# Where the FFN's order starts and ends: weight splits, down units and the final norm moved in the instruction order of a one-core encoder step

## The chip, the core and the metric

The program runs on one core of one Trainium2 chip. Its engines work at the same time and each takes its own instructions in order: PE multiplies matrices, with its weight loads shown apart as PEld; DVE works elementwise; ACT copies, scales and applies functions; POOL is a slower third elementwise engine; and SP's queue issues most of the transfers. The metric is the device time of one execution in microseconds; the median of three runs before is 843.84 us (840.65 to 845.9).

## What is computed

One layer of a hybrid encoder over a token block of 544 columns: 32 sample tokens, then 512 prompt tokens (meta tokens are dropped before this part). After the attention branches:

```
h = h + einsum('btd,de->bte', m, w_out)
u = einsum('btd,df->btf', rmsnorm(h, norm_ffn), w_up)      # 1024 -> 4096
h = h + einsum('btf,fd->btd', square(relu(u)), w_down)     # 4096 -> 1024
y = rmsnorm(h, norm_final)
```

The work this case is about lies between the product with `w_out` and the output of `y`: the feed-forward network (FFN), from about 443 us to the end.

## The kernel before

**Values in two parts.** Every operand of a large product is split into a high part (rounded by ACT, line 121) and a low part (the rest, subtracted by DVE, line 124), and a product is three matmuls: high with high, high with low, low with high. Names ending in `h` or `hi` are high parts, in `l` or `lo` low parts (`whi`/`wlo`, `hh`/`hl`, `uh`/`ul`, `dh`/`dl`, `lh`/`ll`).

**The up products (`up_pair`, line 1365).** The 4096 rows of u are made in 16 pairs of 128. A pair is a 2x2 block product over halves of the 1024 inputs and halves of the 544 tokens, done with seven products of 12 matmuls (128x272) in place of eight. In order they take the weights a11, s1, s2, s4, s3, a12, a22 (the s are sums and differences of blocks, made by DVE from the raw `wr`) and the operand combinations B11, BM, BN, B22, BT3, B21, BT4 in `hh`/`hl`. They accumulate in three PSUM tiles, `ps_x`, `ps_v` and `ps_y`, and ACT copies a partial result out (`fa`, `fb`, `x`) before the next product adds to the same tile, so that product waits for the copy. `up_pair` is a generator with seven steps, n = 0 to 6; the program does other work between its steps. `pair_prep` (line 263) is the generator that loads and splits a pair's weights, one step ahead; pair 0 is prepared while the last two `w_out` products run.

**The operands (`operands`, line 1231).** The eight 128-row parts d of h come out of the `w_out` loop in the order 0, 4, 1, 5, 2, 6, 3, 7 (line 1272): DVE adds the product to `xres`, ACT and DVE scale it, combine the halves and split into `hh`/`hl`. The last part's combinations (`b`, `bb`, `ba`) are what the third product of pair 0 waits for.

**The down products (`down`, line 1441).** The up pairs are grouped into eight chunks, `CHUNKS`, of 1, 2, 2, 2, 2, 2, 2 and 3 pairs. For every chunk c there are eight units d: 128 rows of the output times the chunk's u, in two column ranges of 288 and 256 tokens (`OC`). The units of chunk c-1 are put between the steps n = 1, 3, 5, 6 of the first two pairs of chunk c (lines 1492 to 1503). Their weights are loaded into `dr` and split by `down_prep` (line 326). Chunk 0's results are copied to `acc` by ACT; `square` (line 1472) adds up the squares of h, and `norm2` (line 1481) makes the FFN norm's factor `r2` from them with two small matmuls `ps_r`.

**The last chunk (lines 1509 to 1554).** Chunk 7 has 18 matmuls per unit and column range. The eight units run over the first 288 columns, then over the last 256. Units 0 and 1 use the `whi`/`wlo` buffers that the up weights used before, units 2 to 7 new ones (`lh`/`ll`). `last_evac` multiplies by `r2` (`dt`) and adds to `hs` (`xres`). `final_part` (line 1313) transposes h on PE (`ps_fin`), squares it on ACT (`fj`) and multiplies by the norm's weight on DVE (`ytok`); T0 is the first three token tiles, T1 the last two, and the parts 0, 1, 2 cover d = 0 to 3, 4 to 6 and 7. `final_norm` scales the rows and sends them out.

**What sets the order.** From line 1205 on PE, ACT and DVE run their instructions in the order in which the program's source issues them. SP's and POOL's order is chosen by a scheduler. A buffer of a pool is given to its next tile when the last reader of the former tile is done.

Of the kernel before, what the change touches and what calls it, by code (L numbers as in the profile page):

```python
# [15 lines left out]
P = 128  # L16
# [31 lines left out]
def tile_hybrid_step(  # L48
# [185 lines left out]
    def unit_prep(n):  # L234
        key, parts = units[n]
        raw = wpool.tile([P, KD, P], F32, tag="raw", name=f"wr_{n}", bufs=3)
        k = 0
        for src in parts:
            kk = src.shape[0] // P
            SP.dma_start(raw[:, k: k + kk, :], src.rearrange("(k p) n -> p k n", p=P))  # L240
            k += kk
        if parts[0].shape[0] == D and key[0] in IN_KEYS:
            POOL.tensor_tensor(raw, raw, gmix.unsqueeze(2).to_broadcast([P, KD, P]), ALU.mult)  # L243
        hi = wpool.tile([P, KD, P], F32R, tag="whi", name=f"wh_{n}", bufs=2)
        lo = wpool.tile([P, KD, P], F32R, tag="wlo", name=f"wl_{n}", bufs=2)
        split_hi(hi, raw)
        split_lo(lo, raw, hi)
        done[key] = (hi, lo)
# [14 lines left out]
    def pair_prep(g):  # L263
# [47 lines left out]
        if g == 0:  # L311
            for i, nm in enumerate(("s2", "s4")):
                split(one(nm), 0, [nm], s24[:, i: i + 1])
        else:
            B = t(wpool, "whi", bufs=2), t(wpool, "wlo", bufs=2)
            split(B, 0, ["s2", "s4"], s24)
# [955 lines left out]
    for n, d in enumerate(WO_ORDER):  # L1272
        xr = tmp([TM], f"xres{d}")
        POOL.tensor_tensor(xr, xh[:, d, M0:].bitcast(F32), xl[:, d, M0:].bitcast(F32), ALU.add)
        wh, wl = use(("wo", d))
        if n == KD - 2:
            prep = pair_prep(0)
            go(prep, 3)
        if n == KD - 1:
            go(prep, 4)  # L1280

        def evac_o(ci, a, b, ps, xr=xr):
            DVE.tensor_tensor(xr[:, a:b], ps, xr[:, a:b], ALU.add)

        blocks(f"wo{d}", range(KD), wh, wl, lambda k, a, b: mh[k][:, a:b], lambda k, a, b: ml[k][:, a:b],
               OC, evac_o, psany, both=n == 0)
        hs[d] = xr
        operands(d, n == KD - 1)
# [76 lines left out]
    def up_pair(g):  # L1365
# [13 lines left out]
        if g == 0:  # L1379
# [3 lines left out]
            drain(own)  # L1383
# [6 lines left out]
        ACT.activation(fb[:, 1, :], vv, AF.Copy)  # L1390
        yield
        product(X, W["s2"], BN, False)
        ACT.activation(fa[:, 1, :], xv, AF.Copy)
        go(prep, 1)
# [46 lines left out]
    def down(i):  # L1441
        c, d = dn[i]
        if i + 1 < len(dn):
            go(dpreps[i + 1], 1)
# [44 lines left out]

    dstart(0)  # L1490
    dstart(1)
    for c in range(NCH):
        for jj, g in enumerate(CHUNKS[c]):
            for n, _ in enumerate(up_pair(g)):
                if c == 0 and n == 5:
                    go(dpreps[0], 1)
                if c > 0 and jj < 2 and n in (1, 3, 5, 6):
                    d = 4 * jj + (1, 3, 5, 6).index(n)
# [3 lines left out]
                    if c == 2 and d == 2:  # L1502
                        norm2()
    while tail:
        tail.pop(0)()
# [5 lines left out]
    def last(d, a, b, psf):  # L1511
        wh, wl = downs[c, d]
        ps = psf(f"ps_dn{c}_{d}_{a}")
        K = 2 * len(CHUNKS[c])
        for k in range(K):
# [3 lines left out]
        return ps  # L1519

    def last_evac(d, a, b, ps):
        dt_ = fpool.tile([P, TM], F32, tag="dt", name=f"dt{c}_{d}_{a}", bufs=2)
# [5 lines left out]
    (a, b), T0, T1 = OC[0], range(3), range(3, NTT)  # L1528
    for d in range(KD):
        if d + 1 < KD:  # L1530
            go(dpreps[8 * c + d + 1], 1)
        dstart(8 * c + d + 2)
        ps = last(d, a, b, (psa, pss)[d % 2])
        if d == 4:
            final_part(0, T0)
        rest_a = last_evac(d, a, b, ps)
    a, b = OC[1]
    for d in range(KD):
        ps = last(d, a, b, (psa, pss)[d % 2])
# [7 lines left out]
        if d == 7:  # L1547
            final_part(1, T1)
            final_early(3, NTT)
        rest = last_evac(d, a, b, ps)  # L1550
# [36 lines left out]
```

## Time and profile before

| | us |
|---|---|
| median of three runs | 843.84 |
| lowest, highest | 840.65, 845.9 |
| the profiled execution | 841.46 |
| its span in the trace | 839.7 |

The trace was taken in the profiled execution. Its span runs from the first to the last instruction; the remaining 1.8 us of that execution lie around it. PE is busy for 96% of the span and its weight loads for 92%. The TensorE clock is granted in full except in three places: at the start, from about 451.6 to 458.4 us, and after the last matmul. Engines are shown with the idle time before an instruction and with what ended it; a gap on PE is lost time wherever nothing later absorbs it, while DVE and ACT have many gaps in which they only wait for PE.

### The profile page before, as it was taken

The numbers are of one execution on the slowest core, as the hardware profiler recorded it, in microseconds if no ns is written. First come the engines' busy times: TensorE is split into PE (matmuls) and PEld (weight loads), VectorE is DVE, ScalarE is ACT, GpSimd is POOL, SyncE is SP. The second block draws the span as 40 slices with busy tenths as digits, with TensorE's granted clock in tenths as the row PEclk, the third lists the DMA queues.
The fourth block names the chain that finished last, engine by engine and source line by source line (L and its number), as shares of the span: only waits on it lengthen the run. The fifth ranks groups of instructions, "written<-read, shape, count | busy, mean of one in ns | idle before, by whom it ended". The sixth has DMA issues, their size and how long they took to land.

```text
span 839.7 us, 15161 instructions
## 1 busy us (share of the span) xinstructions
PE 804.4 (96%) x6093; PEld 772.6 (92%) x6093; DVE 585.3 (70%) x1139; ACT 366.2 (44%) x722; POOL 123.3 (15%) x132
## 2 busy tenths in 40 slices
PE   8998999999999999999997999999999999999995
PEld 6867898898999989999997999999999999999995
DVE  5856358798768554466667888776667777798764
ACT  5761454555446523232445673343433344333332
POOL 4305112221121493025000000000000000000000
PEclk8999999999999999999998999999999999999998
DMA  8513223422521132323123142323333333322402
GB/s 244 153 47 100 51 48 98 122 77 59 143 64 51 52 100 77 96 82 101 55 84 115 48 126 73 111 81 90 90 102 101 101 92 98 101 77 63 113 2 107
DMA packets 133813, 75.38 MB, mean 90 GB/s; under 512 B 15056, under 2 KB 129024, under 8 KB 133744
## 3 DMA queue, kind: packets, MB, share of 16 engines
q1 hardware_dynamic: 132704, 72.27, 30.4%
q0 software_dynamic: 1024, 2.14, 1.1%
q8 instruction: 48, 0.79, 0.4%
q14 instruction: 21, 0.17, 0.1%
q10 hardware_dynamic: 16, 0.00, 0.0%
HBM read 69.57 MB, written 4.83 MB: 89 GB/s over the span
## 4 chain that ended last, share of the span: by engine, by line
PE 72%; DVE 13%; ACT 5%; POOL 3%; issue 3%; DMA 3%; SPq 0%; ACTq 0%; POOLq 0%; DVEq 0%
PE ps_dn L118 22%; PE ps_x L118 11%; PE ps_v L118 6%; PE ps_gb L118 5%; PE ps_ga L118 5%; PE ps_fv L118 3%; PE ps_y L118 3%; PE ps_yb L118 2%; PE ps_ya L118 2%; PE ps_wo L118 2%; PE ps_fk L118 2%; DVE wl L124 2%; ACT wh L121 1%; DMA wr<-in_w_in_dram 1%; PE ps_s L118 1%
## 5 line engine op out<-in xcount | busy, mean ns | idle before, releaser
L118 PE MATMUL ps_dn<-uh,dl 128*128 128x288 f32 (+1 forms) x416 | 120.7, 290 | 0.0
L118 PE MATMUL ps_dn<-uh,dh 128*128 128x288 f32 (+1 forms) x416 | 119.7, 288 | 0.9 <-ACT uh L121 0.9
L118 PE MATMUL ps_dn<-ul,dh 128*128 128x288 f32 (+1 forms) x416 | 120.1, 289 | 0.2 <-DVE ul L124 0.2
L121 ACT ACTIVATE wh<-wr 128x1024 fp32r<-128x1024 f32 x46 | 48.5, 1055 | 87.9 <-PE ps_yb L118 24.3
L124 DVE TENSOR_TENSOR wl<-wr,wh 128x1024 fp32r<-128x1024 f32 x46 | 68.7, 1494 | 19.2 <-ACT wh L121 18.8
L118 PEld LDWEIGHTS ps_dn<-uh,dh 128*128 128x128 f32 x416 | 78.5, 189 | 1.1 <-ACT uh L121 1.1
L243 POOL TENSOR_TENSOR wr<-wr,gmix 128x1024 f32<-128x1024 f32 x30 | 58.0, 1937 | 143.2 <-DMA wr<-in_w_in_dram 104.5
L118 PEld LDWEIGHTS ps_dn<-uh,dl 128*128 128x128 f32 x416 | 78.3, 188 | 0.5 <-DVE dl L124 0.5
L118 PEld LDWEIGHTS ps_dn<-ul,dh 128*128 128x128 f32 x416 | 78.3, 188 | 0.5 <-DVE ul L124 0.5
L1468 DVE TENSOR_TENSOR acc<-ps_dn,acc 128x288 f32<-128x288 f32 x96 | 41.1, 438 | 30.4 <-PE ps_dn L118 30.4
L1307 POOL DMA_DIRECT2D gfin<-in_norm_final_dram x1 | 0.6, 607 | 374.1 <-DVE s3l L124 374.1
L118 PE MATMUL ps_x<-hh,whi 128*128 128x272 f32 x124 | 36.1, 291 | 1.5 <-ACT fa L1376 1.3
L124 DVE TENSOR_TENSOR dl<-dr,dh 128x512 fp32r<-128x512 f32 (+1 forms) x56 | 36.3, 648 | 1.7 <-ACT dh L121 1.6
L118 PE MATMUL ps_x<-hh,wlo 128*128 128x272 f32 x124 | 35.9, 290 | 0.5 <-DVE wlo L124 0.5
L118 PE MATMUL ps_v<-hl,whi 128*128 128x272 f32 x124 | 36.0, 290 | 0.0
L118 PE MATMUL ps_v<-hh,whi 128*128 128x272 f32 x124 | 35.8, 289 | 0.0
L118 PE MATMUL ps_x<-hl,whi 128*128 128x272 f32 x124 | 35.8, 289 | 0.0
L118 PE MATMUL ps_v<-hh,wlo 128*128 128x272 f32 x124 | 35.8, 288 | 0.0
L124 DVE TENSOR_TENSOR wlo<-s,whi 128x512 fp32r<-128x512 f32 (+1 forms) x31 | 29.4, 947 | 6.3 <-ACT whi L121 6.3
L935 ACT ACTIVATE sb<-sb,m 128x144 f32<-128x144 f32 (+3 forms) x32 | 18.3, 573 | 35.1 <-DVE m L930 35.1
L121 ACT ACTIVATE dh<-dr 128x512 fp32r<-128x512 f32 (+1 forms) x56 | 33.2, 593 | 0.0
L1403 ACT ACTIVATE x<-ps_x 128x272 f32<-128x272 f32 x16 | 6.4, 397 | 53.2 <-PE ps_x L118 53.1
(511 smaller groups left out, 2467.0 us busy)
## 6 DMA issues: line engine op xcount, KB each, us to landing
wr<-in_w_up_dram SPq DMA_DIRECT2D x62, 256.0 KB, 3.4
wr<-in_w_in_dram SPq DMA_DIRECT2D x30, 512.0 KB, 3.9
dr<-in_w_down_dram SPq DMA_DIRECT2D x48, 256.0 KB, 3.1
wr<-in_w_out_dram SPq DMA_DIRECT2D x8, 512.0 KB, 3.9
dr<-in_w_down_dram SPq DMA_DIRECT2D x8, 384.0 KB, 3.9
cb<-cPd SPq DMA_DIRECT2D x8, 264.0 KB, 4.1
x_t<-in_x_prompt_dram SPq DMA_DIRECT2D x4, 512.0 KB, 5.7
gvraw<-in_w_in_dram SPq DMA_DIRECT2D x4, 512.0 KB, 8.6
```

The costliest lines, as they stand in the source:

```text
L118: return TE.matmul(out, lhsT, rhs, start=start, stop=stop, skip_group_check=True)
L121: ACT.activation(out, in_, AF.Copy)
L124: (eng or DVE).tensor_tensor(out, in_, hi.bitcast(F32), ALU.subtract)
L243: POOL.tensor_tensor(raw, raw, gmix.unsqueeze(2).to_broadcast([P, KD, P]), ALU.mult)
L935: exps.append(ACT.activation(sb, sb, AF.Exp, bias=m, scale=-1.0, accum_out=rs).ins)
L1307: POOL.dma_start(late["gfin"], norm_final.partition_broadcast(P))
L1403: ACT.activation(x3, xv, AF.Copy)
L1468: DVE.tensor_tensor(acc[d][:, a:b], ps[:, :w], acc[d][:, a:b], ALU.add)
```

## The change

The change leaves every instruction of the computation as it is (PE, ACT, DVE, POOL and SP have as many as before) and puts some of them at other places in their engine's order:

- Pair 0: the loads of its weights are issued one `w_out` product earlier in the source, and `s4` is split apart from `s2`; `s4`, `s3`, `a12` and `a22` are split during the pair's own first products.
- Chunk 0's down units: three in pair 1 (n = 3, 5, 6) and five in pair 2 (n = 1, 2, 3, 5, 6), before four and four. `norm2` moves from chunk 2 to chunk 3.
- Last chunk: the weights of units 0 and 1 are loaded and split at steps n = 2 and n = 4 of the last pair; all of unit 0's and unit 1's matmuls but those of the newest u pair's last two k come first; later units' splits are issued one unit earlier in the order; the first part of the final norm is spread over units 4, 5 and 6; and the second part of T1 is put into the middle of the last unit's product.

```diff
--- before.py
+++ after.py
@@ -231,14 +231,21 @@
     def add_unit(key, parts):
         units.append((key, parts))
 
-    def unit_prep(n):
-        key, parts = units[n]
-        raw = wpool.tile([P, KD, P], F32, tag="raw", name=f"wr_{n}", bufs=3)
+    loads = {}
+
+    def unit_load(n):
+        raw = loads[n] = wpool.tile([P, KD, P], F32, tag="raw", name=f"wr_{n}", bufs=3)
         k = 0
-        for src in parts:
+        for src in units[n][1]:
             kk = src.shape[0] // P
             SP.dma_start(raw[:, k: k + kk, :], src.rearrange("(k p) n -> p k n", p=P))
             k += kk
+
+    def unit_prep(n):
+        key, parts = units[n]
+        if n not in loads:
+            unit_load(n)
+        raw = loads.pop(n)
         if parts[0].shape[0] == D and key[0] in IN_KEYS:
             POOL.tensor_tensor(raw, raw, gmix.unsqueeze(2).to_broadcast([P, KD, P]), ALU.mult)
         hi = wpool.tile([P, KD, P], F32R, tag="whi", name=f"wh_{n}", bufs=2)
@@ -309,8 +316,9 @@
         split(A, 1, ["s1"], s31[:, 1:2])
         yield
         if g == 0:
-            for i, nm in enumerate(("s2", "s4")):
-                split(one(nm), 0, [nm], s24[:, i: i + 1])
+            split(one("s2"), 0, ["s2"], s24[:, 0:1])
+            yield
+            split(one("s4"), 0, ["s4"], s24[:, 1:2])
         else:
             B = t(wpool, "whi", bufs=2), t(wpool, "wlo", bufs=2)
             split(B, 0, ["s2", "s4"], s24)
@@ -1273,11 +1281,14 @@
         xr = tmp([TM], f"xres{d}")
         POOL.tensor_tensor(xr, xh[:, d, M0:].bitcast(F32), xl[:, d, M0:].bitcast(F32), ALU.add)
         wh, wl = use(("wo", d))
+        if n == KD - 3:
+            unit_load(nxt[0])
+            prep = pair_prep(0)
+            go(prep, 1)
         if n == KD - 2:
-            prep = pair_prep(0)
+            go(prep, 2)
+        if n == KD - 1:
             go(prep, 3)
-        if n == KD - 1:
-            go(prep, 4)
 
         def evac_o(ci, a, b, ps, xr=xr):
             DVE.tensor_tensor(xr[:, a:b], ps, xr[:, a:b], ALU.add)
@@ -1380,7 +1391,7 @@
 
             own, prep = prep, pair_prep(1)
             go(prep, 1)
-            drain(own)
+            go(own, 1)
         else:
             drain(prep)
             prep = pair_prep(g + 1) if g < 15 else iter(())
@@ -1388,9 +1399,13 @@
         yield
         product(V, W["s1"], BM, True)
         ACT.activation(fb[:, 1, :], vv, AF.Copy)
+        if g == 0:
+            go(own, 1)
         yield
         product(X, W["s2"], BN, False)
         ACT.activation(fa[:, 1, :], xv, AF.Copy)
+        if g == 0:
+            drain(own)
         go(prep, 1)
         yield
         product(V, W["s4"], B22, False)
@@ -1440,7 +1455,7 @@
 
     def down(i):
         c, d = dn[i]
-        if i + 1 < len(dn):
+        if i + 1 < 8 * (NCH - 1):
             go(dpreps[i + 1], 1)
         dstart(i + 2)
         wh, wl = downs.pop((c, d))
@@ -1487,6 +1502,8 @@
             DVE.reciprocal(r2[:, a:b], r2[:, a:b])
 
 
+    REGULAR = [{1: (0,), 3: (1,), 5: (2,), 6: (3,)}, {1: (4,), 3: (5,), 5: (6,), 6: (7,)}]
+    EARLY = [{3: (0,), 5: (1,), 6: (2,)}, {1: (3,), 2: (4,), 3: (5,), 5: (6,), 6: (7,)}]
     dstart(0)
     dstart(1)
     for c in range(NCH):
@@ -1494,13 +1511,15 @@
             for n, _ in enumerate(up_pair(g)):
                 if c == 0 and n == 5:
                     go(dpreps[0], 1)
-                if c > 0 and jj < 2 and n in (1, 3, 5, 6):
-                    d = 4 * jj + (1, 3, 5, 6).index(n)
+                for d in (EARLY if c == 1 else REGULAR)[jj].get(n, ()) if 0 < c and jj < 2 else ():
                     down(8 * (c - 1) + d)
                     if c == 1:
                         square(d)
-                    if c == 2 and d == 2:
+                    if c == 3 and d == 2:
                         norm2()
+                if jj == 2 and n in (2, 4):
+                    go(dpreps[8 * c + n // 2 - 1], 1)
+                    dstart(8 * c + n // 2 + 1)
     while tail:
         tail.pop(0)()
     alloc_ytok()
@@ -1508,35 +1527,58 @@
 
     c = NCH - 1
 
-    def last(d, a, b, psf):
+    K = 2 * len(CHUNKS[c])
+
+    def last(d, ci, ps, ks):
+        a, b = OC[ci]
         wh, wl = downs[c, d]
-        ps = psf(f"ps_dn{c}_{d}_{a}")
-        K = 2 * len(CHUNKS[c])
-        for k in range(K):
+        for k in ks:
             uh, ul = u_tile(c, k)
             for m, (w_, x_) in enumerate(((wh, uh), (wl, uh), (wh, ul))):
                 mm(ps[:, : b - a], w_[:, k, :], x_[:, a:b], k == 0 and m == 0, k == K - 1 and m == 2)
-        return ps
-
-    def last_evac(d, a, b, ps):
-        dt_ = fpool.tile([P, TM], F32, tag="dt", name=f"dt{c}_{d}_{a}", bufs=2)
+
+    def last_ps(d, ci):
+        return (psa, pss)[d % 2](f"ps_dn{c}_{d}_{ci}")
+
+    def last_evac(d, ci, ps):
+        a, b = OC[ci]
+        dt_ = fpool.tile([P, TM], F32, tag="dt", name=f"dt{c}_{d}_{ci}", bufs=2)
         DVE.tensor_tensor(dt_[:, : b - a], ps[:, : b - a], r2[:, a:b], ALU.mult)
         if d < KD - 1:
             DVE.tensor_tensor(hs[d][:, a:b], hs[d][:, a:b], dt_[:, : b - a], ALU.add)
         return dt_, a
 
-    (a, b), T0, T1 = OC[0], range(3), range(3, NTT)
+    def prep_last(d):
+        if d < KD:
+            go(dpreps[8 * c + d], 1)
+            dstart(8 * c + d + 2)
+
+    T0, T1 = range(3), range(3, NTT)
+
+    first = [last_ps(d, 0) for d in range(2)]
+    for d in range(2):
+        last(d, 0, first[d], range(K - 2))
+    prep_last(2)
     for d in range(KD):
-        if d + 1 < KD:
-            go(dpreps[8 * c + d + 1], 1)
-        dstart(8 * c + d + 2)
-        ps = last(d, a, b, (psa, pss)[d % 2])
-        if d == 4:
-            final_part(0, T0)
-        rest_a = last_evac(d, a, b, ps)
-    a, b = OC[1]
+        if d < 2:
+            ps = first[d]
+            last(d, 0, ps, range(K - 2, K))
+        else:
+            ps = last_ps(d, 0)
+            last(d, 0, ps, range(K))
+        rest_a = last_evac(d, 0, ps)
+        prep_last(d + 3)
+        if 4 <= d < 7:
+            final_part(0, [d - 4])
     for d in range(KD):
-        ps = last(d, a, b, (psa, pss)[d % 2])
+        ps = last_ps(d, 1)
+        if d < KD - 1:
+            last(d, 1, ps, range(K))
+        else:
+            last(d, 1, ps, range(3))
+            final_part(1, T1)
+            last(d, 1, ps, range(3, K))
+            final_early(3, NTT)
         if d == 0:
             final_part(1, T0)
         if d == 1:
@@ -1544,10 +1586,7 @@
             final_early(0, 3)
         if d == 5:
             final_part(0, T1)
-        if d == 7:
-            final_part(1, T1)
-            final_early(3, NTT)
-        rest = last_evac(d, a, b, ps)
+        rest = last_evac(d, 1, ps)
         if d == 2:
             final_norm(0, 3)
     final_part(2, T1, rest)
```

**ACT, pair 0.** From the split of `s2` to the copies after the first two products; `b` and `hh` are the last operand part, `fa` and `fb` the copies out of `ps_x` and `ps_v`. Before:

```order
L121 ACTIVATE s2h_5176<-s_0_5106 128x512
L121 ACTIVATE s4h_5180<-s_0_5106 128x512
L121 ACTIVATE s3h_5184<-s_0_5104 128x512
L1252 ACTIVATE b_5240<-xres_5168,prmT 128x544
L121 ACTIVATE hh_4671<-bb_5162 128x544
L1376 ACTIVATE fa_5267<-ps_x_5269 128x272
L121 ACTIVATE hh_4671<-b_5240 128x544
L121 ACTIVATE hh_4671<-ba_5161 128x272
L121 ACTIVATE a12h_5296<-wr_0_5099 128x512
L121 ACTIVATE a22h_5300<-wr_0_5098 128x512
L1390 ACTIVATE fb_5268<-ps_v_5270 128x272
L1393 ACTIVATE fa_5267<-ps_x_5269 128x272
```

With the change:

```order
L121 ACTIVATE s2h_5176<-s_0_5106 128x512
L1260 ACTIVATE b_5232<-xres_5168,prmT 128x544
L121 ACTIVATE hh_4671<-bb_5162 128x544
L1387 ACTIVATE fa_5259<-ps_x_5261 128x272
L121 ACTIVATE hh_4671<-b_5232 128x544
L121 ACTIVATE hh_4671<-ba_5161 128x272
L121 ACTIVATE s4h_5288<-s_0_5106 128x512
L1401 ACTIVATE fb_5260<-ps_v_5262 128x272
L121 ACTIVATE s3h_5305<-s_0_5104 128x512
L1406 ACTIVATE fa_5259<-ps_x_5261 128x272
L121 ACTIVATE a12h_5322<-wr_0_5030 128x512
L121 ACTIVATE a22h_5326<-wr_0_5029 128x512
```

`s4h` and `s3h` have moved behind the operand's splits, and `s3h`, `a12h` and `a22h` behind the copy `fb`. On DVE the subtractions `s4l` and `s3l` have moved in the same way, from ahead of the last `xres` to behind the last `hl`.

**ACT, last pair.** `whi_0` and `whi_1` are the high weights of down units 0 and 1 of the last chunk, `fa` and `fb` with the higher numbers the copies of pair 15, `uh` the split of u. Before:

```order
L1417 ACTIVATE fb_8952<-ps_x_8953 128x272
L121 ACTIVATE whi_0_9202<-dr_0_9144 128x768
L1376 ACTIVATE fa_9242<-ps_x_9244 128x272
L121 ACTIVATE uh_8949<-fb_8952 128x544
L121 ACTIVATE a22h_9261<-wr_15_8974 128x512
L1390 ACTIVATE fb_9243<-ps_v_9245 128x272
L1393 ACTIVATE fa_9242<-ps_x_9244 128x272
L1403 ACTIVATE x_15_9316<-ps_x_9244 128x272
L121 ACTIVATE uh_9240<-fa_9242 128x544
L1417 ACTIVATE fb_9243<-ps_x_9244 128x272
L121 ACTIVATE uh_9240<-fb_9243 128x544
L121 ACTIVATE whi_1_9364<-dr_1_9206 128x768
```

With the change:

```order
L1432 ACTIVATE fb_8952<-ps_x_8953 128x272
L1387 ACTIVATE fa_9238<-ps_x_9240 128x272
L121 ACTIVATE uh_8949<-fb_8952 128x544
L121 ACTIVATE a22h_9257<-wr_15_8974 128x512
L1401 ACTIVATE fb_9239<-ps_v_9241 128x272
L1406 ACTIVATE fa_9238<-ps_x_9240 128x272
L121 ACTIVATE whi_0_9287<-dr_0_9144 128x768
L1418 ACTIVATE x_15_9318<-ps_x_9240 128x272
L121 ACTIVATE whi_1_9321<-dr_1_9202 128x768
L121 ACTIVATE uh_9236<-fa_9238 128x544
L1432 ACTIVATE fb_9239<-ps_x_9240 128x272
L121 ACTIVATE uh_9236<-fb_9239 128x544
```

`whi_0` has moved from ahead of pair 15's first copy to behind its third, and `whi_1` from behind the last `uh` to ahead of the last two. On DVE `wlo_0` and `wlo_1` have moved likewise; `wlo_1` now stands between the copies' additions for the fifth and the sixth product.

**DVE, last chunk, first column range.** `dt` and `xres` belong to the unit named by their number, `ll` is the low part of a unit's weights, `ytok` the first part of the final norm. Before:

```order
L1525 TENSOR_TENSOR xres_5090<-xres_5090,dt_3_0_9473 128x288
L124 TENSOR_TENSOR ll_5_9477<-dr_5_9452,lh_5_9476 128x768
L1329 TENSOR_TENSOR ytok_9359<-ps_fin_0_9501,gfin 32x512
L1329 TENSOR_TENSOR ytok_9360<-ps_fin_1_9509,gfin 128x512
L1329 TENSOR_TENSOR ytok_9361<-ps_fin_2_9517,gfin 128x512
L1523 TENSOR_TENSOR dt_4_0_9525<-ps_dn_4_0_9482,r_5257 128x288
L1525 TENSOR_TENSOR xres_4743<-xres_4743,dt_4_0_9525 128x288
L124 TENSOR_TENSOR ll_6_9529<-dr_6_9480,lh_6_9528 128x768
```

With the change:

```order
L1548 TENSOR_TENSOR xres_5098<-xres_5098,dt_3_0_9481 128x288
L124 TENSOR_TENSOR ll_6_9485<-dr_6_9432,lh_6_9484 128x768
L1546 TENSOR_TENSOR dt_4_0_9507<-ps_dn_4_0_9488,r_5249 128x288
L1548 TENSOR_TENSOR xres_4743<-xres_4743,dt_4_0_9507 128x288
L124 TENSOR_TENSOR ll_7_9511<-dr_7_9460,lh_7_9510 128x768
L1340 TENSOR_TENSOR ytok_9367<-ps_fin_0_9514,gfin 32x512
L1546 TENSOR_TENSOR dt_5_0_9541<-ps_dn_5_0_9522,r_5249 128x288
L1548 TENSOR_TENSOR xres_4881<-xres_4881,dt_5_0_9541 128x288
L1340 TENSOR_TENSOR ytok_9368<-ps_fin_1_9544,gfin 128x512
```

The splits stand two units ahead of their use where they stood one unit ahead, and the three `ytok` are spread over three units.

## Rows read from the trace of the kernel before

**Rows 1.** Page, section 1: busy us of each engine, share of the span, instructions

```profile
PE 804.4 (96%) x6093; PEld 772.6 (92%) x6093; DVE 585.3 (70%) x1139; ACT 366.2 (44%) x722; POOL 123.3 (15%) x132
```

**Rows 2.** Waits of PE, 385 to 840 us: us in total, times, longest

```profile
PE ps_x L118 <- ACT fa L1376: 3.9, 2, 2.7
PE ps_fin L118 <- DVE dt L1523: 1.8, 1, 1.8
PE ps_dn L118 <- ACT uh L121: 1.5, 2, 0.9
PE ps_dn L118 <- DVE ll L124: 1.0, 1, 1.0
PE ps_v L118 <- ACT fb L1390: 0.9, 1, 0.9
PE ps_r L118 <- DVE r L1486: 0.6, 1, 0.6
```

**Rows 3.** Timeline, pairs 0 and 1: start us, us, instruction, [idle <- releaser]

```profile
446.22 0.69 DVE L124 TENSOR_TENSOR s4l<-s,s4h 128x512 fp32r<-128x512 f32 x1
...
447.43 0.78 DVE L1283 TENSOR_TENSOR xres<-ps_wo,xres 128x288 f32<-128x288 f32 x2
...
453.99 0.37 ACT L1390 ACTIVATE fb<-ps_v 128x272 f32<-128x272 f32 x1
...
459.96 0.44 DVE L1404 TENSOR_TENSOR fb<-x,fb 128x272 f32<-128x272 f32 x1 [0.78 <-ACT x L1403]
460.91 1.23 DVE L124 TENSOR_TENSOR wlo<-s,whi 128x1024 fp32r<-128x1024 f32 x1 [0.51 <-ACT whi L121]
...
465.34 0.72 DVE L1418 SCALAR_TENSOR_TENSOR fb<-fb 128x544 f32<-128x544 f32 x1
...
467.18 0.38 ACT L1390 ACTIVATE fb<-ps_v 128x272 f32<-128x272 f32 x1
...
468.99 0.65 ACT L1475 ACTIVATE r<-xres 128x544 f32<-128x544 f32 x1
...
470.03 0.29 PE L118 MATMUL ps_v<-hh,whi 128*128 128x272 f32 x1
```

**Rows 4.** Busy time of 452 to 458 us: engines, then PEclk, DMA share, GB/s

```profile
452.00:458.00 6.00, 5.12 (x23) 4.80 (x23) 5.21 (x10) 3.19 (x7) 0.00 (x0) 0.50 0.46 135
```

**Rows 5.** Chain of waits that ended last: start us, us, what, instructions

```profile
471.70 1.50 PE ps_dn L118 x12
473.21 1.51 PE ps_x L118 x12
...
802.63 7.02 PE ps_dn L118 x53
...
814.40 8.41 PE ps_dn L118 x72
```

**Rows 6.** Timeline, last pair and first units of the last chunk

```profile
774.47 0.29 PE L118 MATMUL ps_v<-hl,whi 128*128 128x272 f32 x1
...
774.84 0.84 ACT L121 ACTIVATE whi<-dr 128x768 fp32r<-128x768 f32 x1 [5.76 <-PE ps_v L118]
...
776.02 0.40 PE L118 MATMUL ps_x<-hh,whi 128*128 128x272 f32 x1 [1.26 <-ACT fa L1376]
...
783.67 0.30 PE L118 MATMUL ps_dn<-uh,whi 128*128 128x288 f32 x1
...
790.49 0.29 PE L118 MATMUL ps_dn<-uh,lh 128*128 128x288 f32 x1
```

**Rows 7.** Timeline of DVE, last chunk, the sixth weight split

```profile
801.62 0.95 DVE L124 TENSOR_TENSOR ll<-dr,lh 128x768 fp32r<-128x768 f32 x1
```

**Rows 8.** Timeline of DVE at the end of the last product

```profile
828.97 1.03 DVE L1329 TENSOR_TENSOR ytok<-ps_fin,gfin 128x384 f32<-128x384 f32 x2 [2.09 <-ACT fj L1328]
...
830.18 0.42 DVE L1523 TENSOR_TENSOR dt<-ps_dn,r 128x256 f32<-128x256 f32 x1
```

**Rows 9.** Page, section 6, DMA issues: tile, queue, count, KB each, us to landing

```profile
dr<-in_w_down_dram SPq DMA_DIRECT2D x8, 384.0 KB, 3.9
```

## The prediction

> **What bounds the kernel now.** I read the page first, then the waits of PE over the part that the change touches, then the timeline around each long wait, then the granted clock there and the chain that ended last. The page says that PE is busy for 96% of the span [rows 1], and the change removes no matmul, so the only time to be had is PE's idle time. The list of PE's waits says where it is [rows 2]: 3.9 us in two waits for the copy `fa`, 1.5 us in two waits for `uh`, 0.9 us for the copy `fb`, 1.0 us for a weight split `ll`, 1.8 us for the last `dt`, and 0.6 us inside `norm2`. The reader is to see that each releaser is ACT or DVE, never a transfer: these engines take their work in order, and something stood ahead of what PE needed. The timeline shows what.
>
> An idle entry is smaller than the time lost. A matmul is listed at 0.29 us and overlaps the next: twelve take 1.51 us [rows 5], 0.126 each, and the first after a pause is listed at 0.40 [rows 6]. So a pause costs its entry plus about 0.16, plus 0.1 for the slow restart.
>
> **The change part by part.**
>
> *Pair 0 and pair 1.* Today DVE starts `s4l` at 446.22 and the last `xres` at 447.43 [rows 3]: the two subtractions `s4l` and `s3l` hold up the last operand part by 1.21 us, and with it `b`, `bb`, `hh` and the third product, which has the longest wait (2.7 of the 3.9 us). With the change that chain is 1.21 us earlier, and so is the copy `fb` of 453.99 [rows 3], which has one ACT split ahead of it in place of two; the wait of 0.9 us behind it goes too. But this is not yet the gain, since the work only moved: both subtractions now come behind the last `hl`, and each waits for its ACT split, so DVE begins pair 1 about 0.4 us later than now. What DVE gets back are its own waits, 0.78 us before 459.96 and 0.51 us before 460.91 [rows 3], and a smaller one. Walking its queue in the new order with the old durations, I get the `wlo` of 460.91 at 459.8 (it then waits only for ACT's split), and everything behind it 1.1 us earlier: the `fb` of 465.34 at 464.2, and ACT's copy `fb` of 467.18 at 466.1, done at 466.45. PE's next must is that copy, since the down unit that used to wait for `uh` in front of it (0.9 of the 1.5 us) now stands behind it. So PE starts this product at 466.5. Today it starts at 470.03 [rows 3], with one down unit done that now follows, 1.50 us [rows 5]. The gain is 470.03 - 1.50 - 466.5 = **2.0 us**.
>
> The clock does not enter this term. From 452 to 458 us PE was granted 0.50 of full speed, the 1.2 GHz level [rows 4], after the 2.7 us pause, and those 6 us at half speed cost 3.0. If the same low stretch stays, PE reaches the copy of 466.45 at 465.4 to 466.0; if it goes, PE arrives up to 3 us earlier and waits. The copy decides either way. The ends for this term are -1.0 (a low stretch of the same size comes after 466.5 instead, where nothing absorbs it) and 5.0 (DVE and ACT do not hold PE, and the low stretch is gone). I take 2.0, as the walk rests on rows of the same instructions.
>
> *Down units of chunk 0.* Five units in pair 2 make it twelve blocks of 1.5 us on PE, 18 us. Per unit ACT has a split, two copies and a square (the square 0.65 [rows 3]); I estimate 1.5 us, so 7.5, beside 6 to 7 for the pair itself. It fits: **0**. If it did not, the copies that PE waits for would be late (a rival below). `norm2` takes its wait of 0.6 [rows 2] to the same place of the next chunk: **0**.
>
> *Loads of pair 0.* SP's order and what each load waits for are the same in both programs up to the first down weights, because a load waits for its buffer, not for its place in the source. **0**.
>
> *Hand-over to the last chunk, first half.* ACT takes `whi` at 774.84 after idling 5.76 us: its buffer still belongs to pair 15's first weights, which PE reads until its second product ends. The copy `fa` behind it is needed for the third product, which starts at 776.02 where it was due at 774.47 + 0.13 = 774.60 [rows 6]. With the restart this costs 1.5 us. With the change `whi` stands behind the third copy, when the buffer is long free. The gain is **1.5 us**. The loads of units 0 and 1 need no more time: their buffers come free with the last pair's own splits, as now.
>
> *Hand-over, second half.* Units 0 and 1 take from 783.67 to 790.49, 6.82 us, for 36 matmuls [rows 6] that at 7.02 / 53 = 0.1325 [rows 5] need 4.77: 2.05 us are lost to the last half of u (0.6 of the `uh` waits) and to `wlo` of unit 1. With the change the first twelve matmuls of unit 1, 1.6 us, stand before the last half of u, and both splits are done. What is late next: `wlo_1`, about 0.95 us like the `ll` of [rows 7], stands on DVE ahead of the addition for the fifth or sixth product, and pushes the last `ul` by about 0.55, to 0.1 or 0.2 us after PE wants it. So the gain is **1.9 us**; the ends are 1.0 (all of `wlo_1` on the path) and 2.05.
>
> *First column range.* At 801.62 [rows 7] `ll` starts behind three `ytok`, and PE waits 1.0 us for it [rows 2]. With the change it stands two units ahead, 2 x 18 x 0.1325 = 4.8 us. The price is two more restarts for the transposes that are now in three places: 1.0 + 0.16 + 0.1 - 0.2 = **1.1 us**. Each unit's load waits for the split three units before it and lands in 3.9 us [rows 9]; with about 1.8 us of split the cycle is 5.7 for three units, against 7.2 on PE, so loads stay hidden. If that cover were gone, a unit would cost 1 to 2 us more.
>
> *The end.* DVE starts the two `ytok` of part 1 at 828.97 and the last `dt` at 830.18, behind them [rows 8]; PE waits 1.8 us for it. Nine matmuls now follow the transposes, 9 x 8.41 / 72 = 1.05 us [rows 5], so ACT and DVE start that much earlier. PE's work ahead of the wait is the same in sum, so the wait shrinks from 1.8 to 0.8 and DVE still sets the end: **1.05 us**.
>
> The sum is 2.0 + 1.5 + 1.9 + 1.1 + 1.05 = 7.5 us. Against the profiled execution of 841.46 this is 834.0. That execution lies 2.4 us under the median of 843.84; the four executions known (840.65, 841.46, 843.84, 845.9) have a mean of 843.0, and 843.0 - 7.5 = 835.5.
>
> **The rivals.**
>
> *The low clock comes later, 838.5.* If the clock holds at 452 us, PE runs ahead and idles up to 3 us around 461 to 466.5, as long as the pause that preceded the fall [rows 2, 4]. A fall there costs the 3.0 us of [rows 4] with nothing to absorb it: 7.5 - 3.0 = 4.5. For it: the pauses are no shorter in sum. Against: they are split into shorter ones, and the 1.26 us pause of [rows 6] left the clock up. The Trainium skill (TensorE: Matmul & The Clock Gate, What's actually happening) has it that "the default state is throttled, and activity releases the throttle"; by that rule a PE that idles less is likelier to keep the clock, and [rows 4, 6] agree.
>
> *PE is not held in pair 1, 832.5.* If my walk of DVE's queue is too long and the clock holds, the first term is 5.0 in place of 2.0. Against: the walk leaves DVE one short wait in this stretch, and its durations are those of [rows 3].
>
> *Slower, 847.* ACT in pair 2 of chunk 1. Five squares and ten copies stand among the copies that PE needs; if each unit makes PE wait as it did for `uh` (0.9 us, 1.16 with overlap and restart) and the clock then falls twice (2 x 3.0), that is 5.8 + 6.0 = 11.8 us, against 7.5: 4 us slower. It decides from the point where a unit costs ACT more than the 1.5 us that PE gives it beside its product's 1.5. Today a unit costs about 1.5 of 3.0, so this is unlikely.
>
> *Most of it does nothing, 839.5.* Every wait removed shows up behind the next in-order neighbour; I let half of the sum survive, 3.7.
>
> **How the numbers follow.** The forecast has 0.68, the later fall of the clock 0.13, PE not held 0.06, half the sum 0.10, slower 0.03. The predicted time is that of the forecast, 835.5. Its own range is 833 to 838 (terms 1 us either way, three-run medians 1.5 to 2). For 8 in 10 I go from 831.5, which takes in most of the faster case, to 840. A change of under 1% (8.4 us) is about what a measurement here can't tell from none, the three runs spreading 0.6%. Faster by over 1% of 843.84 means under 835.4: nearly half of the forecast, 0.33, the faster case and a little of the rest, 0.42 in all. Within 1%: 0.55. Slower: 0.03.
>
> **What would show it.** In the trace after: no PE wait for `fa` over 2 us in pair 0 and none in pair 15; the fourth product of pair 1 waiting for `fb` and nothing before its first down unit; `ps_dn` of units 0 and 1 of the last chunk in about 4.9 us; no wait for `ll`; a last wait for `dt` of 0.8. I am wrong if PE shows new waits in pairs 1 and 2, if the granted clock is low after 460 us, or if the last `uh` still holds up unit 0 by more than 0.5 us.

## The result and the profile after

The changed kernel takes 838.24 us (median of 19 runs, 832.98 to 841.42) against 843.84 for the kernel before (19 runs beside it, 839.69 to 847.2): a ratio of 0.9938, 95% interval 0.9921 to 0.9956, so 0.6% faster. Two more comparisons gave 0.9903 (0.9869 to 0.9936) and 0.9892 (0.9854 to 0.9929). All 32 executions of it in the three comparisons have a mean of 837.0, all 79 of the kernel before, beside these and the runs below, 843.6: 6.6 us, with a standard error of 0.5. The forecast was 835.5 and a gain of 7.5.

The profiled execution took 834.47 us, its span 832.6. The page's row of engines, beside [rows 1]: the same 6093 matmuls in a shorter span.

```profile
PE 803.6 (97%) x6093; PEld 771.7 (93%) x6093; DVE 584.2 (70%) x1139; ACT 366.8 (44%) x722; POOL 123.8 (15%) x132
```

The waits of PE in the same part as [rows 2] (us in total, times, longest):

```profile
PE ps_v L118 <- ACT fb L1401: 2.4, 2, 1.3
PE ps_x L118 <- ACT fa L1387: 1.7, 2, 1.5
PE ps_fin L118 <- DVE dt L1546: 0.8, 1, 0.8
PE ps_v L118 <- DVE fa L1425: 0.6, 1, 0.6
PE ps_r L118 <- DVE r L1501: 0.6, 1, 0.6
```

The waits for `uh` and `ll` are gone, the one for `fa` in pair 15 too, and the last `dt` costs 0.8 in place of 1.8. What is left lies in pairs 0 and 1, in shorter pieces. PE's timeline there, of [rows 3] and later (start us, us, instruction, idle before and releaser):

```profile
444.97 0.39 PE L118 MATMUL ps_x<-hh,whi 128*128 128x272 f32 x1 [0.25 <-ACT whi L121]
450.44 0.40 PE L118 MATMUL ps_x<-hh,s2h 128*128 128x272 f32 x1 [1.47 <-ACT fa L1387]
453.36 0.39 PE L118 MATMUL ps_v<-hh,s4h 128*128 128x272 f32 x1 [1.15 <-ACT fb L1401]
462.13 0.40 PE L118 MATMUL ps_v<-hh,whi 128*128 128x272 f32 x1 [0.64 <-DVE fa L1425]
467.19 0.39 PE L118 MATMUL ps_v<-hh,whi 128*128 128x272 f32 x1 [1.27 <-ACT fb L1401]
```

The window of [rows 4], after (engines' busy time, then clock, DMA share, GB/s): the clock is 1.00 where it was 0.50.

```profile
452.00:458.00 6.00, 4.80 (x36) 4.38 (x35) 5.17 (x9) 4.47 (x10) 0.00 (x0) 1.00 0.29 86
```

The two traces do not enter the FFN at the same time, so I measure everything from pair 0's first product (444.97 above). Four marks of the changed kernel: pair 15's first product, the first unit of the last chunk, its third, and the second column range; the fifth is the last row of PE's timeline that waits.

```profile
770.06 0.29 PE L118 MATMUL ps_x<-hh,whi 128*128 128x272 f32 x1
780.63 0.30 PE L118 MATMUL ps_dn<-uh,whi 128*128 128x288 f32 x1
785.67 0.29 PE L118 MATMUL ps_dn<-uh,lh 128*128 128x288 f32 x1
801.28 0.28 PE L118 MATMUL ps_dn<-uh,whi 128*128 128x256 f32 x1
823.57 0.49 PE L118 MATMUL ps_fin<-ident,dt 128*128 128x128 f32 x2 [0.79 <-DVE dt L1546]
```

The marks of the kernel before that [rows 6] do not hold:

```profile
444.31 0.39 PE L118 MATMUL ps_x<-hh,whi 128*128 128x272 f32 x1 [0.27 <-ACT whi L121]
771.58 0.29 PE L118 MATMUL ps_x<-hh,whi 128*128 128x272 f32 x1
807.36 0.28 PE L118 MATMUL ps_dn<-uh,whi 128*128 128x256 f32 x1
830.65 0.49 PE L118 MATMUL ps_fin<-ident,dt 128*128 128x128 f32 x2 [1.84 <-DVE dt L1523]
```

The differences of these starts, part by part:

| part | before | after | gain | forecast |
|---|---|---|---|---|
| pair 0 to pair 15 | 327.27 | 325.09 | 2.18 | 2.0 |
| pair 15 | 12.09 | 10.57 | 1.52 | 1.5 |
| units 0 and 1 | 6.82 | 5.04 | 1.78 | 1.9 |
| rest of the first column range | 16.87 | 15.61 | 1.26 | 1.1 |
| second column range, to the last `dt` | 23.29 | 22.29 | 1.00 | 1.05 |

That is 7.7 us against a forecast of 7.5, and each line agrees. But the timed runs gain 6.6 in the mean and 5.6 by the first medians, and the experiments show that the first line agrees for a wrong reason.

### The profile page after: what moved, and what is told of

It is laid out like the page before. It is cut to its first block, busy times and chain, and to the rows that moved or that the text cites. A ratio compares the mean times of both kernels' runs of the same rounds, so it can differ in the third digit from the quotient of the medians.

```text
span 832.6 us, 15162 instructions
## 1 busy us (share of the span) xinstructions
PE 803.6 (97%) x6093; PEld 771.7 (93%) x6093; DVE 584.2 (70%) x1139; ACT 366.8 (44%) x722; POOL 123.8 (15%) x132
## 4 chain that ended last, share of the span: by engine, by line
PE 73%; DVE 12%; ACT 5%; DMA 3%; POOL 3%; issue 3%; SPq 0%; ACTq 0%; POOLq 0%; DVEq 0%
PE ps_dn L118 23%; PE ps_x L118 11%; PE ps_v L118 5%; PE ps_gb L118 5%; PE ps_ga L118 5%; PE ps_fv L118 3%; PE ps_y L118 3%; PE ps_yb L118 3%; PE ps_ya L118 3%; PE ps_wo L118 2%; PE ps_fk L118 2%; DMA wr<-in_w_in_dram 2%; DVE wl L124 2%; ACT wh L121 1%; PE ps_s L118 1%
## 5 line engine op out<-in xcount | busy, mean ns | idle before, releaser
L121 ACT ACTIVATE whi<-s 128x512 fp32r<-128x512 f32 (+1 forms) x31 | 25.8, 832 | 6.5 <-DVE s L315 3.9
```

Source lines behind the costliest of these rows:

```text
L121: ACT.activation(out, in_, AF.Copy)
```

## Experiments

**The changed kernel again, twice.** No edit.

> The changed kernel itself, beside the three others on one chip. The two profiled executions differ by 7.1 us (841.46 to 834.47 with clock means of 0.988 and 0.993), the medians by 5.6 (ratio 0.9938). Theory C, the clock: the terms of the sum are right, but in most executions of the changed kernel PE falls to the lower level for some 6 us somewhere, which its profiled execution did not; then an execution's time goes with its clock mean (0.001 is about 0.84 us), and executions at 0.993 or more stand 7 us or more under those of the kernel before at 0.988. Theory P, a part is smaller: the time does not go with the clock mean, and the parts below add up to about 5.5 at any clock. Both: ratio 0.992 to 0.995.

Median 837.45 against 844.25, ratio 0.9903 (0.9869 to 0.9936). In its trace the clock is 1.00 all through pairs 0 and 1, the pauses are the same to 0.01 us, and from pair 0 to the end of the span it takes 387.69 us, the first trace 387.63. So theory C has no low stretch in the FFN to point at, and the clock means that it compares do not count the same stretches in every execution (last section).

> The changed kernel beside the best version on one chip. By the traces it gains 6.2 us on the kernel before where the clock holds in both (5.55 in the last chunk, 0.65 at the start), 7.7 where the clock falls in pair 0 of the kernel before: ratio 0.991 to 0.993. From pair 0's first product to the end of the span 387.65 us.

Median 836.33 against 845.65, ratio 0.9892 (0.9854 to 0.9929). Pair 0 to pair 15 is 325.09 once more. To the end it takes 388.01 where 387.65 was expected: here the rest of the first column range is 15.93 us in place of 15.61.

**The two halves of the change alone.** The first keeps the table of down units and pair 0's steps, and has the kernel before's last chunk (cut, against the changed kernel):

```diff
-        if i + 1 < 8 * (NCH - 1):
+        if i + 1 < len(dn):
...
-                if jj == 2 and n in (2, 4):
-                    go(dpreps[8 * c + n // 2 - 1], 1)
-                    dstart(8 * c + n // 2 + 1)
```

(and the block behind the loop as before); the second is the kernel before with those lines and the new block.

> Only the start of the FFN is changed: weights and operands of pairs 0 and 1, down units of the first chunk, place of the norm; the last chunk is as before. By the trace of the changed kernel this part gives 1.5 us (pair 15's first product starts 1.52 earlier). Theory C: 1.5 to 2.2 by the trace where no stretch of the FFN is at the lower level, but 0 or up to 1.5 slower by the median, as the low stretch of 452 to 458 us of the kernel before cost nothing (the copy hid it) and one in the changed order costs up to 3. Theory P: 1.5 to 2 by trace and median. The pauses of pairs 0 and 1 are as in the changed kernel: 1.5, 1.2, 0.6, 0.3 and 1.3 us.

> Only the last chunk is changed: weight splits of its first units after the third copy of pair 15, units 0 and 1 in two halves, splits two units ahead in the first column range, transposes spread, last product cut at the transposes; the start is as before. Sum of the four terms: 1.5 + 1.9 + 1.1 + 1.05 = 5.55 us. Theory C: 5.5 by trace and median (nothing here touches the stretch where the clock falls). Theory P with the loss in this part: 3.5 to 4, and a wait in the last chunk that the changed kernel's profile did not show.

The start alone: 842.99 against 844.25, ratio 0.9984 (0.9960 to 1.0008), no difference that this shows; 325.09 from pair 0 to pair 15. The end alone: 839.49, ratio 0.9961 (0.9940 to 0.9981), 4.8 us by the medians. Its trace holds the answer to the first line of the table. It has the kernel before's start, instruction for instruction, but its clock did not fall there. PE's first product, the wait for `uh` of [rows 2], and pair 15:

```profile
449.32 0.39 PE L118 MATMUL ps_x<-hh,whi 128*128 128x272 f32 x1 [0.27 <-ACT whi L121]
...
470.32 0.40 PE L118 MATMUL ps_dn<-uh,dh 128*128 128x288 f32 x1 [0.93 <-ACT uh L121]
...
775.06 0.29 PE L118 MATMUL ps_x<-hh,whi 128*128 128x272 f32 x1
```

775.06 - 449.32 is 325.74, not 327.27: the low stretch of [rows 4] cost 1.53 us, though I had it hidden. To the end of the span it takes 388.48. With the clock held, then, the start gains 325.74 - 325.09 = 0.65 us.

ACT and DVE tell why. ACT's copy `x`, for which DVE waits 0.78 in [rows 3], first in the trace of before, then with the end changed alone:

```profile
459.53 0.40 ACT L1403 ACTIVATE x<-ps_x 128x272 f32<-128x272 f32 x1 [2.84 <-PE ps_x L118]
```

```profile
462.74 0.40 ACT L1403 ACTIVATE x<-ps_x 128x272 f32<-128x272 f32 x1 [1.04 <-PE ps_x L118]
```

The DVE instruction of 459.96 and the `wlo` of 460.91 in [rows 3], with the end changed alone:

```profile
463.83 0.43 DVE L1404 TENSOR_TENSOR fb<-x,fb 128x272 f32<-128x272 f32 x1
464.44 1.23 DVE L124 TENSOR_TENSOR wlo<-s,whi 128x1024 fp32r<-128x1024 f32 x1 [0.17 <-ACT whi L121]
```

Both of DVE's waits, 0.78 and 0.51, go to 0 and 0.17 with no change to the order. They were waits for PE at half speed, handed on by ACT.

What the order does to the copy `fb` of pair 1, and to PE's fourth product behind it, can be read at a held clock too. The copy and the product with the end changed alone (old start), then the copy in the changed kernel, whose product of 467.19 stands above:

```profile
470.70 0.38 ACT L1390 ACTIVATE fb<-ps_v 128x272 f32<-128x272 f32 x1
...
473.55 0.29 PE L118 MATMUL ps_v<-hh,whi 128*128 128x272 f32 x1
```

```profile
466.76 0.38 ACT L1401 ACTIVATE fb<-ps_v 128x272 f32<-128x272 f32 x1
```

From pair 0's first product the copy comes at 21.38 in the old order and at 21.79 in the new one, 0.41 us later and not earlier. PE's product comes at 24.23 in the old order, with one down unit of 1.50 us done, and at 22.22 in the new one: 24.23 - 1.50 - 22.22 = 0.51 us of gain. It comes although the copy is later, since the unit that waited for `uh` (0.93) no longer stands in front.

**Is the fall of the clock a habit?** The kernel before once more:

> The kernel before once more, for a second trace. Measured from pair 0's first product (444.31 us in the first trace) its parts are 327.27 us to pair 15, 395.39 to the end of the span; with only the last chunk changed the same start took 325.74, at 1.00 of the clock throughout. Theory L: the low stretch of 452 to 458 us belongs to that one execution, and the kernel before needs 325.7 to pair 15 and 393.9 to the end without it; the changed kernel (387.65 in both traces) then gains 6.2 us and not 7.7. Theory S: the stretch comes with the pause of 2.7 us in most executions: 327.3 and 395.4 again.

Theory S here: the clock falls again, and pair 15 starts 327.17 us behind pair 0. The clock of 451.6 to 458.4 us in this trace:

```profile
451.60:458.40 6.80, 6.00 (x27) 5.68 (x26) 6.00 (x11) 3.19 (x7) 0.00 (x0) 0.51 0.52 146
```

So of three traces with this start two fell and one held, on the same pause of 2.67 us. What decides between them is not shown.

**Fill the pauses.** Matmuls that nothing reads, ahead of the products that wait:

```diff
+        if g == 0:
+            fill(9, BM)
         product(X, W["s2"], BN, False)
...
+        if g < 2:
+            fill(7 + g, BN)
         product(V, W["s4"], B22, False)
```

> The changed kernel with 9 matmuls (128x128, 272 columns, into a PSUM bank that nothing reads) ahead of pair 0's third product, 7 ahead of its fourth and 8 ahead of pair 1's fourth, 0.126 us each, in pauses of 1.5, 1.15 and 1.27 us: they add 0.0 to 0.3 us of work to the path. Theory C with the fall of the clock in these pauses: the median goes down by 1.5 to 3 us against the changed kernel, clock mean up by 0.002 to 0.004. Theory P, or a fall elsewhere: the same as the changed kernel, or up to 0.5 slower.

837.63, ratio 0.9916 (0.9885 to 0.9948), the changed kernel beside it 837.45 (means of seven executions each 836.4 and 835.9); 387.69 us from pair 0 to the end. The times show no gain, and no trace of either has a low stretch in the FFN: nothing is left that speaks for theory C. The same in the kernel before (19 and 11 matmuls):

> The kernel before with matmuls that nothing reads in its two pauses of pair 0: 19 ahead of the third product (2.67 us), 11 ahead of the fourth (1.67 us where the clock held), 0.126 us each; nothing else differs. In two traces of the kernel before the clock fell behind the first pause (452 to 458 us), in the third execution with this start it held. Theory F (the pause lets the clock fall, in some executions): no low stretch between pair 0 and pair 15, 325.7 us from one to the other and 393.9 to the end; median lower by up to 1.5 us, by as much as falls are frequent. Rival (the fall has to do with something else): a low stretch there as before, 327.2 and 395.3.

The clock held and pair 15 came 325.74 us behind pair 0, as theory F says; but the time is that of the kernel before, ratio 1.0004 (0.9975 to 1.0033). The trace shows what a held clock gives. It does not show that filling held it, since the clock held once without (the end alone), and the times, with an interval of 2.4 us either way, do not show that the fall was common enough for filling to pay. How often it falls stays open.

**Which part of the start gains.** The down units of the first chunk back at their old steps:

```diff
-                for d in (EARLY if c == 1 else REGULAR)[jj].get(n, ()) if 0 < c and jj < 2 else ():
+                for d in REGULAR[jj].get(n, ()) if 0 < c and jj < 2 else ():
```

> The changed kernel, but with the down units of the first chunk where they were: four in pair 1, four in pair 2. Theory O (the order of the units carries what the start gains): unit 0 waits for the last half of u ahead of pair 1's third product, 0.9 to 1.4 us, and from pair 0's first product to pair 15 it takes 325.7 to 326.0 us, where the changed kernel takes 325.1. Theory W (the earlier operands and weights carry it): the pause only moves from pair 1's fourth product to the unit, 325.0 to 325.2.

> A second look at the changed kernel with the first chunk's down units where they were. In the first look the clock fell at 464.3 to 467.7 us, inside pair 1, and pair 15 came 327.26 us behind pair 0. That is 3.4 us at half speed, 1.7 us, so 325.6 where the clock holds by theory O (order of the units: 0.5 us of the 0.65 that the start gains); theory W has 325.1 to 325.2. If the clock falls again, 327.2 again, and the question stays.

In both executions the clock fell inside pair 1: 327.26 and 327.63 us to pair 15. PE's waits and the clock in the first:

```profile
463.11 0.40 PE L118 MATMUL ps_dn<-ul,dh 128*128 128x288 f32 x1 [0.89 <-DVE ul L124]
464.44 0.61 PE L118 MATMUL ps_dn<-uh,dh 128*128 128x288 f32 x1 [0.92 <-ACT uh L121]
```

```profile
464.40:467.60 3.20, 3.17 (x13) 2.91 (x14) 3.15 (x5) 1.98 (x6) 0.00 (x0) 0.50 0.15 43
```

PE was busy through the 3.4 us at half speed, so they cost 1.7, and 325.6 and 325.9 are left: the old start's 325.74. This is an estimate, since no execution of it held the clock; it says that the earlier weights and operands alone gain 0.2 us at most, and that most of the 0.65 hangs on the place of the units, theory O. What that place gains without the earlier weights was not run. What the order did besides: in all eight traces that have it (the changed kernel three times, the start alone, the filled one, and the three below) the clock held in pairs 0 and 1; the order above, with the same longest pause of 1.47 us, lost it twice.

**Take the next wait away.** In pair 1 PE waits 1.27 us for ACT's `fb`, which stands behind `uh` and `a22h`. The tail of pair 0, ACT's last `uh` and DVE's `ul` behind it, is issued behind the copy:

```diff
-        while tail:
+        while tail and g != 1:
             tail.pop(0)()
...
         ACT.activation(fb[:, 1, :], vv, AF.Copy)
+        while tail:
+            tail.pop(0)()
```

> The changed kernel with one thing moved: ACT's split uh of pair 0's second half, and DVE's behind it, are issued after the copy fb of pair 1, not ahead of its second product. In the changed kernel PE waits 1.27 us for that copy, which stands behind uh and a22h. Theory A (ACT's order alone holds PE): no wait ahead of pair 1's fourth product, which starts 1.3 to 1.5 us earlier, and the end comes as much earlier (386.2 to 386.4 us from pair 0's first product in place of 387.65). Rival: unit 0 then waits for uh or ul instead, and less than 0.4 is left.

Theory A. PE's third and fourth product of pair 1, the second with no wait:

```profile
466.98 0.39 PE L118 MATMUL ps_x<-hh,whi 128*128 128x272 f32 x1 [0.25 <-ACT fa L1387]
...
468.58 0.30 PE L118 MATMUL ps_v<-hh,whi 128*128 128x272 f32 x1
```

Pair 15 comes 323.52 us behind pair 0, 1.57 earlier, and the end 386.11 behind it.

**A version that beats both.** That move, and the norm's two halves behind units 2 and 3:

```diff
-                    if c == 3 and d == 2:
-                        norm2()
+                    if c == 3 and d in (2, 3):
+                        norm2(d - 2)
```

> The same move, and the norm's two column halves behind units 2 and 3, not both behind unit 2: PE's second product there waits 0.55 us for DVE to empty the one bank, with its restart 0.7 to 0.9. By theory A 1.4 + 0.8 = 2.2 us less than the changed kernel, 385.5 from pair 0's first product; by the rival 0.8 to 1.2. By the clock (runs here spread by 8 us, nearly all of it ahead of pair 0) the ratio to the kernel before comes out at 0.990, give or take 0.003.

> The best version again, timed beside the changed kernel. By the traces 2.2 us less than it (385.45 from pair 0's first product in place of 387.65): ratio 0.988 to 0.990, a median 1 to 3.5 us lower. If what was won at the two places came back as a fall of the clock in most executions, the two medians would be the same.

The norm's two products in the changed kernel, then in this version, 5 us apart and neither waiting:

```profile
559.71 0.65 PE L118 MATMUL ps_r<-r,ones_d 128*128 128x288 f32 x2
...
560.91 0.70 PE L118 MATMUL ps_r<-r,ones_d 128*128 128x256 f32 x2 [0.55 <-DVE r L1501]
```

```profile
562.45 0.65 PE L118 MATMUL ps_r<-r,ones_d 128*128 128x288 f32 x2
...
567.47 0.60 PE L118 MATMUL ps_r<-r,ones_d 128*128 128x256 f32 x2
```

322.73 us to pair 15 and 385.45 and 385.26 to the end, as expected. Medians 834.27 and 835.62, ratios to the kernel before 0.9884 (0.9845 to 0.9923) and 0.9883 (0.9841 to 0.9925). Against the changed kernel the twelve executions have a mean of 834.6 to its 837.0, 2.4 us less with a standard error of 0.9, where the traces say 2.2 to 2.4; beside each other on one chip the two medians were only 0.7 apart, less than the 1 to 3.5 expected, so the times alone would not prove it.

## Why the prediction was right or wrong

*The last chunk.* The four terms were forecast at 1.5 + 1.9 + 1.1 + 1.05 = 5.55 and measured 1.52 + 1.78 + 1.26 + 1.00 = 5.56. The mechanisms are seen: no wait for `fa` in pair 15, units 0 and 1 in 5.04 us, no wait for `ll`, the last `dt` at 0.79. With only this half of the change, it is 393.84 - 388.48 = 5.36 from pair 0 to the end of the span (393.84 is the filled kernel before, the only trace of the old last chunk and the old start at a held clock), the rest of the first column range giving 1.00 there. In the third trace of the changed kernel that part gives 0.94, so the 1.26 of the table is the upper end of what it gives. That the sum agrees to 0.01 is luck: single terms are off by up to 0.16, in both directions.

*Zero for the first chunk's units and for `norm2`.* ACT was not late in pair 2: between the product of 467.19 and the norm's of 560.91 PE has no wait of over 0.15 us, so the slower rival did not come. What the place of the units gains was counted in the first term, and it is most of what that term has. The norm's wait, carried along unchanged at 0.6, was worth 0.79 to the last version when it was taken away.

*Pair 0 and pair 1: the step that failed.* "The clock does not enter this term ... The copy decides either way." For the changed kernel this held. The walk had ACT's copy at 466.1 and PE's product at 466.5, which is 21.8 and 22.2 us behind pair 0's first product of 444.31, and they came at 21.79 and 22.22. What failed is the other side of the difference: today's 470.03 was taken for the old order's time, and 470.03 - 444.31 = 25.72 has the low stretch in it, where the old order at a held clock has 24.23. So the term is 25.72 - 1.50 - 22.22 = 2.00 against the execution that the walk was read from, of which 1.49 is the clock, and 0.51 at a held clock. The walk credited the new order with DVE's waits of 0.78 and 0.51 [rows 3], and their releaser was ACT, so I took them for a matter of order. ACT itself had waited 2.84 us for PE's product, which ran in the low stretch [rows 4]. A row further back would have shown it. Up to pair 15 the size is 0.65 us with the clock held, and 2.18 against an execution of the kernel before that falls; the 3.0 that I had as the price of the low stretch came out at 1.53 there. The bound of 5.0 for this term, with DVE and ACT not holding PE, was far off: PE still waits 1.27 there.

*The sum.* With the clock held it is 0.65 + 5.56 = 6.2, and up to 7.7 where the kernel before falls. The 6.6 us, with its error of 0.5, lies between. The median of 838.24 came out 2.7 above the 835.5, just outside the forecast's own range of 833 to 838 and inside the wider one up to 840. Up to 1.35 of the 2.7 is the first term, the more the rarer the kernel before falls, and 0.6 the base, which was 843.0 from four executions and is 843.6 from 79; the remaining 0.8 or more is of the size of the scatter of medians (the other two were 837.45 and 836.33). That the table's first line reads 2.18 beside 2.0 is no test of the walk's reason: its column before is the same execution that the walk was read from. The rival of a later fall of the clock did not come either, though its 838.5 is near the median: no trace of the changed kernel has a low stretch in the FFN. The Trainium skill's rule that I weighed (TensorE: Matmul & The Clock Gate, What's actually happening), that activity releases the throttle, fits the eight traces of the new start, in which PE idles less and the clock held at 1.00. It does not tell why the old start with its pause of 2.67 us fell twice and held once, nor why the new start with the units at their old steps fell twice with no pause over 1.47. That section of the Trainium skill also says that the number of slow matmuls varies from run to run of one kernel. The traces agree: of the changed kernel's three, one has a low stretch of 6.8 us from 73 us on, one of 10.2 us from 75 us on, and one has none there.

## What to carry to other kernels

When a wait's releaser is itself waiting, follow it until something is busy: a wait for ACT that waits for PE in a stretch of low clock is PE's own time, and a new order does not win it. Before a saving is put down to an order, measure each part from a mark inside the program in two or three traces: 0.65 us and 1.53 us of clock stood here in one difference of 2.18. And where PE waits for a short copy, look at what stands ahead of it in the copying engine's order: moving one split behind one copy gave 1.57 us, more than the whole rearranged start.

## What the runs showed of the chip

Most of the spread between executions arises ahead of the FFN, in a part that is nearly the same in all these kernels. Pair 0's first product starts anywhere from 442.29 us (a third trace of the changed kernel) to 449.86 (the filled kernel before), while from there to the end equal programs agree within 0.4 us where the clock held. The largest piece is the clock of about 75 to 86 us, where PE is busy throughout. With the end changed alone, pair 0 at 449.32, the window 76 to 82 us and PE at two marks around the stretch:

```profile
76.00:82.00 6.00, 6.00 (x33) 4.57 (x30) 2.43 (x8) 0.00 (x0) 0.00 (x0) 0.50 0.35 90
...
63.18 0.22 PE L706 MATMUL ps_lfa<-ident,lf_tok 64*8 64x64 f32 x1
...
88.10 0.32 PE L118 MATMUL ps_oS<-qsS,states 128*128 128x64 f32 x1
```

The third trace of the changed kernel, pair 0 at 442.29:

```profile
76.00:82.00 6.00, 6.00 (x52) 5.58 (x50) 2.71 (x10) 0.49 (x1) 2.69 (x2) 1.00 0.39 108
...
61.05 0.22 PE L714 MATMUL ps_lfa<-ident,lf_tok 64*8 64x64 f32 x1
...
81.50 0.32 PE L118 MATMUL ps_oS<-qsS,states 128*128 128x64 f32 x1
```

From one mark to the other it takes 24.92 us with the low stretch and 20.45 without: 4.5 us. Four of the fourteen traces have no low stretch there, and they start pair 0 at 442.3 to 444.3; in the first trace of the changed kernel it is shorter (23.20 us between the marks, pair 0 at 444.97); the other nine start pair 0 at 447.25 to 449.86.

At the start a printed clock of 1.00 can mislead. The window of 8 to 14 us in the second trace of the kernel before, then with the end changed alone:

```profile
8.00:14.00 6.00, 5.27 (x22) 5.27 (x23) 5.29 (x11) 4.93 (x12) 3.41 (x11) 0.50 1.04 272
```

```profile
8.00:14.00 6.00, 5.36 (x23) 5.05 (x22) 5.07 (x11) 4.94 (x12) 3.61 (x12) 1.00 1.05 265
10.28 0.43 PE L118 MATMUL ps_g<-g1h,xh 128*128 128x280 f32 x1
14.19 0.29 PE L118 MATMUL ps_g<-g1h,xh 128*128 128x280 f32 x1
```

PE does as many matmuls in both, and the same matmul takes 0.43 us at 10.28 and 0.29 at 14.19, so PE ran slow there in the second trace too, under a clock shown as 1.00. The mean clock of an execution therefore counts this stretch in some executions and leaves it out in others, and is no measure of what the FFN got.

Medians of these kernels mix such executions, so a difference of a few microseconds in the FFN is better read from marks in the traces than from the times.
